# FFN up projection: x's hi and lo halves as one 512-column moving operand, gate product on GpSimd

## Chip, cores and metric

The kernel runs on one core of one Trainium2 chip. The metric is the device time of one execution in microseconds, as the median of several runs. The kernel before takes 886.51 us (3 runs, 885.42 to 887.31).

## The reference

A trunk of two decoder layers on 256 tokens of width 1024, all in float32. Each layer does token mixing (latent attention and sparse attention side by side), cross-attention into 256 memory tokens, and a gated feed-forward block (FFN) with a causal depthwise convolution, each followed by a layer norm. The change is in the FFN:

```
def conv_ffn(x, w_up, conv_w, conv_b, w_down):      # x (1,256,1024), w_up (1024, 2*2816), w_down (2816, 1024)
    u = x @ w_up
    u = causal depthwise conv of width 3 over u, + conv_b
    a, g = split(u, 2, axis=-1)
    return (a * silu(g)) @ w_down
```

## The kernel before

**Numbers as hi and lo.** TensorE multiplies in a rounded 32-bit format (float32r). To keep float32 precision every operand v is split: hi is v rounded, made by a copy on ScalarE (L130 for weights), and lo = v - hi, made by a subtraction on VectorE (L131). A product is then three matmuls accumulated in PSUM: hi·hi, hi·lo and lo·hi. Weights come in pieces of 128x1024 numbers (512 KB): SyncE starts the DMA into one of 4 "raw" buffers (L122), and the two halves go into rings of 6 "hi" and 6 "lo" buffers.

**The activation.** x lies transposed in two tiles, xTh and xTl, each [128, 2 token tiles, 8 contraction tiles, 128 tokens] (`new_xT`, L253). `transposed` (L242 to L251) fills them after each layer norm, one token tile after the other, by PE transposes into PSUM, a ScalarE copy for hi and a VectorE subtraction for lo. Cross-attention's values xv reuse the two slots (L873).

**The FFN.** The 2816 hidden columns are 22 tiles of 128 (index f), each with a part a and a gate part g. `up_piece(j)` (L925) serves f = 2j and 2j+1 for j = 0 to 10. It loads and splits four weight pieces (two for a, two for g). For each f and each part it runs `mm_tr` (L173 to L179): for each of the 8 contraction tiles three matmuls of 256 columns, with the weights stationary (hi, hi, lo) and x moving (hi, lo, hi). Both parts of an f share one PSUM bank. Then come, for each part, bias and the current tap on ScalarE (L953), two earlier taps on VectorE (L954, L955), all reading u from PSUM, and for the pair silu on ScalarE (L957), the gate product on VectorE (L958), the hi copy on ScalarE (L960) and the lo subtraction on VectorE (L961). `down_piece(f)` multiplies the result with w_down: 12 matmuls of 512 columns for one f (L970 to L972), accumulated in four PSUM banks that stay open for the whole FFN.

**Order.** The loop at L983 runs up_piece(j) and then down_piece for f = 2j-2 and 2j-1, so that the elementwise work of one pair has the next pair's up matmuls to hide behind. The last five f are summed up in a tail. In layer 1 the first j goes the "natural" way (L929 to L936): x is stationary and the weights move, token tile 0 first, while token tile 1 is still in its layer norm; the result is transposed back (L945). The framework derives all waits from the tiles' views and orders each engine's queue by its own planning; each engine runs its queue in order.

**PSUM.** Eight banks, in two groups of four: group a holds the open accumulators, group b the up results ("up") and the layer norm's transposes ("lnt"), among others.

Of the kernel before, what the change touches and what calls it, by code (L numbers as in the profile page):

```python
# [10 lines left out]
F32 = mybir.dt.float32  # L11
F32R = mybir.dt.float32r
BF16 = mybir.dt.bfloat16
AF = mybir.ActivationFunctionType
ALU = mybir.AluOpType
# [3 lines left out]
P = 128  # L19
D = 1024  # L20
S = 256
DEPTH = 2
NT = S // P
KD = D // P
# [9 lines left out]
NF = DFF // P  # L34
# [55 lines left out]
def trunk(ctx: ExitStack, tc: tile.TileContext, a: dict, out: bass.AP):  # L90
    nc = tc.nc
    V, A, G, T = nc.vector, nc.scalar, nc.gpsimd, nc.tensor
# [3 lines left out]
    big = ctx.enter_context(tc.tile_pool(name="big", bufs=1))  # L96
    tmp = ctx.enter_context(tc.tile_pool(name="tmp", bufs=2))
# [5 lines left out]
    def bank(kind):  # L103
        tag = cfg['bank'][kind]
        return ps_.tile([P, 512], F32, name=kind, tag=tag, bufs=BUFS[tag])

    def loadc(name, shape, dtype=F32):
        t = const.tile(shape, dtype, name=name, tag=name)
        nc.sync.dma_start(t, a[name])
        return t  # L110
# [4 lines left out]
    RAW, HL, PP = SIZES  # L115
# [18 lines left out]
    def wmat(w, cuts, ks=KD, cols=None, wn=None):  # L134

        n = sum(c1 - c0 for c0, c1 in cuts)
        per = max(1, 1024 // (wn or n))
        out_ = []
        for k0 in range(0, ks, per):
            k1 = min(ks, k0 + per)  # L140
            segs, o = [], 0
            for c0, c1 in cuts:
                segs.append(((0, k1 - k0), (o, o + c1 - c0),
                             w[k0 * P:k1 * P, c0:c1].rearrange("(k p) n -> p k n", p=P)))
                o += c1 - c0
            h, lo = piece(k1 - k0, n, segs, wn, cols)
            out_ += [(h[:, i], lo[:, i]) for i in range(k1 - k0)]
        return out_
# [13 lines left out]
    def split(hl, x):  # L162
        A.activation(hl[0], x, AF.Copy)
        V.tensor_tensor(hl[1], x, hl[0].bitcast(F32), op=ALU.subtract)

    def mm_nat(o, xh_, xl_, t, ws):

        for k, (h, lo) in enumerate(ws):
            T.matmul(o, xh_[:, t, k], h, start=k == 0, stop=False)  # L169
            T.matmul(o, xh_[:, t, k], lo, start=False, stop=False)  # L170
            T.matmul(o, xl_[:, t, k], h, start=False, stop=k == len(ws) - 1)  # L171

    def mm_tr(o, xh_, xl_, ws, m0):  # L173

        ms = slice(m0, m0 + P)
        for k, (h, lo) in enumerate(ws):
            T.matmul(o, h[:, ms], xh_[:, :, k], start=k == 0, stop=False)  # L177
            T.matmul(o, h[:, ms], xl_[:, :, k], start=False, stop=False)  # L178
            T.matmul(o, lo[:, ms], xh_[:, :, k], start=False, stop=k == len(ws) - 1)  # L179
# [16 lines left out]
    ident = loadc("c_ident", [P, P])  # L196
# [45 lines left out]
    def transposed(x, t, xh, xl):  # L242
        for c in range(2):
# [6 lines left out]
            A.activation(h, pv, AF.Copy)  # L250
            V.tensor_tensor(xl[:, t, 4 * c:4 * c + 4], pv, h.bitcast(F32), op=ALU.subtract)  # L251

    def new_xT():  # L253
        return [big.tile([P, NT, KD, P], F32R, name="xT" + s, tag="xT" + s) for s in "hl"]

    warm(8, 256)
    gb = []
    for i in range(2):
        gb.append([bank("fill") for _ in range(2)])
        for c in range(2):  # L260
            T.matmul(gb[i][c], ones[0:1, 0:P].bitcast(F32), rows[:, i, c * 512:(c + 1) * 512], start=True, stop=True)
    xh, xl = new_xT()
    for t in range(NT):
        layer_norm(xn[t], gb, act=cfg['lnact']['in'][t])
# [29 lines left out]
    def pcol(name, l, i, n=1):  # L294
        r0, r = PAR[name]
        c = r0 + l * r + i
        return par[:, c:c + n]
# [85 lines left out]
    for l in range(DEPTH):  # L383
# [296 lines left out]
        def ch_transposed():  # L680
            ch = new_xT()
            for k in range(5):
                pb = bank("cht")
                for t in range(NT):
                    T.transpose(pb[:, t * P:(t + 1) * P], cqn[:, t, k * P:(k + 1) * P], ident)
                gcol = pcol("cqg", l, k) if k < 3 else pcol("ckvg", l, k - 3)
                pv = pb[:, 0:S].rearrange("p (t n) -> p t n", t=NT)
                A.activation(ch[0][:, :, k], pv, AF.Copy, scale=gcol)
                V.scalar_tensor_tensor(ch[1][:, :, k], pv, gcol, ch[0][:, :, k].bitcast(F32),
                                       op0=ALU.mult, op1=ALU.subtract)  # L690
            return ch
# [134 lines left out]

        accs = proj(wout, oh, ol)
        xh, xl = new_xT()
        for t in range(NT):
            residual_ln(accs, t, gb, "1")  # L830
# [4 lines left out]
        qx, vx, pTx = {}, [], []  # L835
# [34 lines left out]

        def xa_v(i):
            if not vx:
                vx.extend(big.tile([P, NT, D], F32R, name="xv" + s, tag="xT" + s) for s in "hl")  # L873
            v, *hl = [x[:, :, i * 256:(i + 1) * 256] for x in (kvs[l].v, *vx)]
            if i in kvs[l].vwork:
                kvs[l].vwork.pop(i)(hl)
            else:
                split(hl, v)
# [23 lines left out]
        for i in range(4):  # L902
            steps[f"q{i}"] = lambda i=i: xa_q(i)
            steps[f"qk{i}"] = lambda i=i: xa_qk(i)
            steps[f"v{i}"] = lambda i=i: xa_v(i)
            steps[f"av{i}"] = lambda i=i: xa_av(i)
# [4 lines left out]
        xh, xl = new_xT()  # L911
# [13 lines left out]
        def up_piece(j):  # L925
            wsa = wmat(wup, [(j * 256, (j + 1) * 256)])
            wsg = wmat(wup, [(DFF + j * 256, DFF + (j + 1) * 256)])
            nat = []
            if j < cfg['natural']:  # L929
                nt = big.tile([P, NT, 512], F32, name="nat", tag="k1")  # L930
                for t in range(NT):
                    pb = bank("nat")
                    for s, ws in enumerate((wsa, wsg)):
                        mm_nat(pb[:, s * S:(s + 1) * S], xh, xl, t, ws)
                    A.activation(nt[:, t, :], pb, AF.Copy)
                    nat.append(nt[:, t, :])  # L936
            for i in range(2):
                f = 2 * j + i
                pb = bank("up")
                conv = []  # L940
                for s, ws in enumerate((wsa, wsg)):
                    if nat:
                        for t in range(NT):
                            c0 = s * S + t * P
                            T.transpose(pb[:, c0:c0 + P], nat[t][:, s * S + i * P:s * S + (i + 1) * P], ident)  # L945
                    else:
                        mm_tr(pb[:, s * S:(s + 1) * S], xh, xl, ws, i * P)
                for s in range(2):
                    ft = s * NF + f
                    u = pb[:, s * S:(s + 1) * S]  # L950
                    c = tmp.tile([P, S], F32, name="cv", tag=("pp", "pT")[s], bufs=(PP, 4)[s])
                    w_ = [pcol("cw", l, tap * 2 * NF + ft) for tap in range(3)]
                    A.activation(c, u, AF.Identity, bias=pcol("cb", l, ft), scale=w_[2])  # L953
                    V.scalar_tensor_tensor(c[:, 1:], u[:, :S - 1], w_[1], c[:, 1:], op0=ALU.mult, op1=ALU.add)  # L954
                    V.scalar_tensor_tensor(c[:, 2:], u[:, :S - 2], w_[0], c[:, 2:], op0=ALU.mult, op1=ALU.add)  # L955
                    conv.append(c)
                A.activation(conv[1], conv[1], AF.Silu)  # L957
                V.tensor_tensor(conv[0], conv[0], conv[1], op=ALU.mult)  # L958
                fh, fl = fr[0][:, f % KD, :], fr[1][:, f % KD, :]
                A.activation(fh, conv[0], AF.Copy)  # L960
                V.tensor_tensor(fl, conv[0], fh.bitcast(F32), op=ALU.subtract)  # L961
                down[f] = fh, fl

        def down_mm(f, w_, t, c):
# [18 lines left out]
        for j in range(NF // 2):  # L983
            up_piece(j)
            if j == 0:
                accs.update({(t, c): bank(f"acc{t}") for t in range(NT) for c in range(2)})
            for f in (2 * j - 2, 2 * j - 1):
                if 0 <= f < NF - cfg['last']:
                    down_piece(f)
# [9 lines left out]
        if l + 1 < DEPTH:  # L999
            xh, xl = new_xT()  # L1000
# [35 lines left out]
```

## Time and profile before

| | us |
|---|---|
| median of 3 runs | 886.51 (885.42 to 887.31) |
| the profiled execution | 884.51 |
| its span on the core | 882.7 |
| PE busy / VectorE / ScalarE / GpSimd | 866.8 / 660.4 / 511.2 / 39.9 |
| FFN of layer 0, of layer 1 (up matmuls first to last, plus tail) | 271 to 458, 684 to 875 |
| granted TensorE clock, mean | 0.997 |

Durations of matmuls overlap, since they are pipelined: a matmul of 256 columns is shown as 0.28 us, but the next one starts 0.12 us later. The pace is read from the start times.

### The profile page before, as it was taken

To read this page: it belongs to the slowest core of one execution; us is meant where nothing else is said; L and a number is where in the kernel's file an instruction comes from. 1 tells how busy PE (TensorE), PEld (TensorE's weight loads), DVE (VectorE), ACT (ScalarE), POOL (GpSimd) and SP (SyncE) were. 2 spreads that over 40 slices of the span, in tenths; PEclk is the share of its full clock that TensorE was granted. 3 is DMA by queue.
4 is the path that set the end of the run, shared out by engine and by line. 5 is a ranking of instruction groups with operands and counts; after the bars stand their busy time and mean duration, and the time that the engine had idled before them with its cause. 6 is when DMAs were issued, how large, how long until landed. Compare 5 with 4: busy or idle time off the path is not lost.

```text
span 882.7 us, 15902 instructions
## 1 busy us (share of the span) xinstructions
PE 866.8 (98%) x6110; PEld 798.4 (90%) x6110; DVE 660.4 (75%) x1294; ACT 511.2 (58%) x938; POOL 39.9 (5%) x60
## 2 busy tenths in 40 slices
PE   9989999999999999999999999999999999999996
PEld 6989788899989999999989998879998999999995
DVE  7799886756687777677688798858666777667767
ACT  5659764546445655465556678636573465555551
POOL 1052000000000000000000020000000000000000
PEclk9999999999999999999999999999999999999999
DMA  8953372584257556556539634546632756646631
GB/s 235 284 151 111 128 191 96 164 256 154 96 154 243 177 188 205 179 172 202 177 119 240 178 94 105 144 143 218 193 117 95 239 156 198 205 159 192 214 120 48
DMA packets 128240, 148.72 MB, mean 168 GB/s; under 512 B 6260, under 2 KB 111010, under 8 KB 128164
## 3 DMA queue, kind: packets, MB, share of 16 engines
q1 hardware_dynamic: 128159, 147.70, 54.4%
q8 instruction: 48, 0.79, 0.4%
q14 instruction: 29, 0.23, 0.1%
q10 hardware_dynamic: 4, 0.01, 0.0%
HBM read 146.64 MB, written 1.05 MB: 167 GB/s over the span
## 4 chain that ended last, share of the span: by engine, by line
PE 91%; DVE 4%; ACT 2%; DMA 1%; issue 1%; SPq 0%; POOL 0%; DVEq 0%; ACTq 0%; POOLq 0%
PE up L179 9%; PE up L178 9%; PE up L177 9%; PE acc L970 5%; PE acc L971 5%; PE acc L972 5%; PE acc L170 3%; PE acc L169 3%; PE acc L171 3%; PE fill L179 2%; PE fill L178 2%; PE xq L179 2%; PE xq L178 2%; PE xq L177 2%; PE fill L171 2%; PE fill L169 2%
## 5 line engine op out<-in xcount | busy, mean ns | idle before, releaser
L131 DVE TENSOR_TENSOR lo<-raw,hi 128x1024 fp32r<-128x1024 f32 (+5 forms) x296 | 320.2, 1094 | 81.6 <-ACT hi L130 77.2
L130 ACT ACTIVATE hi<-raw 128x1024 fp32r<-128x1024 f32 (+5 forms) x296 | 279.1, 955 | 149.7 <-PE acc L171 34.7
L179 PE MATMUL up<-xTh,lo 128*128 128x256 f32 x672 | 190.2, 283 | 0.0
L178 PE MATMUL up<-xTl,hi 128*128 128x256 f32 x672 | 190.2, 283 | 0.0
L177 PE MATMUL up<-xTh,hi 128*128 128x256 f32 x672 | 190.2, 283 | 0.0
L178 PEld LDWEIGHTS up<-xTl,hi 128*128 128x128 f32 x672 | 128.9, 192 | 0.7
L177 PEld LDWEIGHTS up<-xTh,hi 128*128 128x128 f32 x672 | 128.9, 192 | 0.7
L179 PEld LDWEIGHTS up<-xTh,lo 128*128 128x128 f32 x672 | 128.9, 192 | 0.0
L954 DVE SCALAR_TENSOR_TENSOR cv<-up,par,cv 128x255 f32<-128x255 f32 x88 | 42.0, 479 | 51.8 <-ACT cv L953 51.8
L953 ACT ACTIVATE cv<-up,par 128x256 f32<-128x256 f32 x88 | 48.8, 557 | 52.8 <-PE up L179 48.3
L971 PE MATMUL acc<-lo,frh 128*128 128x512 f32 x176 | 68.8, 391 | 0.0
L970 PE MATMUL acc<-hi,frh 128*128 128x512 f32 x176 | 68.7, 392 | 0.0
L972 PE MATMUL acc<-hi,frl 128*128 128x512 f32 x176 | 68.2, 389 | 0.0
L571 ACT ACTIVATE p<-p,nm 128x128 f32<-128x128 f32 x96 | 42.7, 447 | 9.5 <-DVE nm L568 9.2
L209 POOL TENSOR_TENSOR mv<-mv,mhalf 128x1 f32<-128x1 f32 x16 | 14.0, 875 | 647.0 <-DVE mv L233 497.1
L955 DVE SCALAR_TENSOR_TENSOR cv<-up,par,cv 128x254 f32<-128x254 f32 x88 | 41.9, 478 | 1.4
L960 ACT ACTIVATE frh<-cv 128x256 fp32r<-128x256 f32 x44 | 18.3, 417 | 37.8 <-DVE cv L958 37.7
L972 PEld LDWEIGHTS acc<-hi,frl 128*128 128x128 f32 x176 | 33.0, 188 | 7.5 <-DVE frl L961 0.6
L970 PEld LDWEIGHTS acc<-hi,frh 128*128 128x128 f32 x176 | 33.1, 188 | 7.0 <-ACT frh L960 0.8
L971 PEld LDWEIGHTS acc<-lo,frh 128*128 128x128 f32 x176 | 33.1, 188 | 6.0
L177 PE MATMUL fill<-mTh,hi 128*128 128x256 f32 x128 | 37.2, 291 | 0.0
L179 PE MATMUL fill<-mTh,lo 128*128 128x256 f32 x128 | 36.6, 286 | 0.0
(270 smaller groups left out, 2015.9 us busy)
## 6 DMA issues: line engine op xcount, KB each, us to landing
raw<-in_ffn_w_up SPq DMA_DIRECT2D x88, 512.0 KB, 4.7
raw<-in_ffn_w_down SPq DMA_DIRECT2D x44, 512.0 KB, 4.5
raw<-in_xa_wkv SPq DMA_DIRECT2D x32, 512.0 KB, 3.3
raw<-in_xa_wq SPq DMA_DIRECT2D x16, 512.0 KB, 5.2
raw<-in_xa_wo SPq DMA_DIRECT2D x16, 512.0 KB, 4.1
raw<-in_w_in SPq DMA_DIRECT2D x24, 256.0 KB, 3.7
raw<-in_w_out SPq DMA_DIRECT2D x16, 256.0 KB, 4.3
raw<-in_w_out SPq DMA_DIRECT2D x8, 512.0 KB
```

What stands on the lines that cost most here:

```text
L130: A.activation(h_, x_, AF.Copy)
L131: V.tensor_tensor(l_, x_, h_.bitcast(F32), op=ALU.subtract)
L169: T.matmul(o, xh_[:, t, k], h, start=k == 0, stop=False)
L171: T.matmul(o, xl_[:, t, k], h, start=False, stop=k == len(ws) - 1)
L177: T.matmul(o, h[:, ms], xh_[:, :, k], start=k == 0, stop=False)
L178: T.matmul(o, h[:, ms], xl_[:, :, k], start=False, stop=False)
L179: T.matmul(o, lo[:, ms], xh_[:, :, k], start=False, stop=k == len(ws) - 1)
L571: A.activation(pc[i], pc[i], AF.Exp, bias=nm[:, i:i + 1], scale=-1.0, accum_out=scs[i])
L953: A.activation(c, u, AF.Identity, bias=pcol("cb", l, ft), scale=w_[2])
L970: T.matmul(o, fh[:, ts_], h[:, cs_], start=f == 0, stop=False)
L971: T.matmul(o, fh[:, ts_], lo[:, cs_], start=False, stop=False)
L972: T.matmul(o, fl[:, ts_], h[:, cs_], start=False, stop=f == NF - 1)
```

## The change

x's tile is now one tile of [128, 8 contraction tiles, hi/lo, 2 token tiles, 128], so that hi and lo of one contraction tile lie side by side as 512 columns; the two old names are views into it. `mm_tr2` runs 8 matmuls with the hi weights and these 512 columns (left half of a full PSUM bank: hi·hi, right half: hi·lo), and then 8 with the lo weights and x's hi (256 columns) into the left half. So one part of one f takes a bank of its own, and the two halves are added up afterwards: ScalarE copies the right half into an SBUF tile u, VectorE adds the left half. The taps then read u from SBUF. The gate product and the lo subtraction go to GpSimd. All of that holds but for the last j (`late`), which stays as it was, save for the layout; layer 1's natural j = 0 keeps its matmuls, and its gate product and subtraction go to GpSimd too. The tile xv becomes one tile in the same slot.

```
+    def mm_tr2(o, x2, ws, m0):
+        ms = slice(m0, m0 + P)
+        for k, (h, lo) in enumerate(ws):
+            T.matmul(o, h[:, ms], x2[:, k], start=k == 0, stop=False)
+        for k, (h, lo) in enumerate(ws):
+            T.matmul(o[:, 0:S], lo[:, ms], x2[:, k, 0], start=False, stop=k == len(ws) - 1)
     def new_xT():
-        return [big.tile([P, NT, KD, P], F32R, name="xT" + s, tag="xT" + s) for s in "hl"]
+        xT = big.tile([P, KD, 2, NT, P], F32R, name="xT", tag="xT")
+        xTs[0] = xT
+        v = xT.rearrange("p k h t n -> p h t k n")
+        return [v[:, 0], v[:, 1]]
...
-                vx.extend(big.tile([P, NT, D], F32R, name="xv" + s, tag="xT" + s) for s in "hl")
+                v2 = big.tile([P, 2, NT, D], F32R, name="xv2", tag="xT")
+                vx.extend([v2[:, 0], v2[:, 1]])
...
+                late = j == NF // 2 - 1
+                if nat or late:
...
+                else:
+                    for s, ws in enumerate((wsa, wsg)):
+                        pb = bank("up")
+                        mm_tr2(pb, xTs[0], ws, i * P)
+                        u = tmp.tile([P, S], F32, name="u", tag=("pp", "pT")[s], bufs=(PP, 4)[s])
+                        A.activation(u, pb[:, S:2 * S], AF.Copy)
+                        V.tensor_tensor(u, pb[:, 0:S], u, op=ALU.add)
+                        us.append(u)
...
-                V.tensor_tensor(conv[0], conv[0], conv[1], op=ALU.mult)
+                E = V if late else G
+                E.tensor_tensor(conv[0], conv[0], conv[1], op=ALU.mult)
...
-                V.tensor_tensor(fl, conv[0], fh.bitcast(F32), op=ALU.subtract)
+                E.tensor_tensor(fl, conv[0], fh.bitcast(F32), op=ALU.subtract)
```

## Rows read from the trace of the kernel before

**Rows 1.** The page: TensorE's busy time, and its granted clock in 40 slices.

```profile
PE 866.8 (98%) x6110; PEld 798.4 (90%) x6110; DVE 660.4 (75%) x1294; ACT 511.2 (58%) x938; POOL 39.9 (5%) x60
PEclk9999999999999999999999999999999999999999
```

**Rows 2.** The page: the chain of waits that ended last, by engine and by line.

```profile
PE 91%; DVE 4%; ACT 2%; DMA 1%; issue 1%; SPq 0%; POOL 0%; DVEq 0%; ACTq 0%; POOLq 0%
PE up L179 9%; PE up L178 9%; PE up L177 9%; PE acc L970 5%; PE acc L971 5%; PE acc L972 5%; PE acc L170 3%; PE acc L169 3%; PE acc L171 3%; PE fill L179 2%; PE fill L178 2%; PE xq L179 2%; PE xq L178 2%; PE xq L177 2%; PE fill L171 2%; PE fill L169 2%
```

**Rows 3.** Windows, FFN stages: length, busy PE, PEld, DVE, ACT, POOL, clock, DMA, GB/s.

```profile
271.00:458.00 187.00, 187.00 (x1323) 175.97 (x1322) 135.81 (x209) 106.27 (x155) 0.92 (x1) 1.00 0.58 184
...
703.00:868.00 165.00, 165.00 (x1168) 155.30 (x1167) 119.50 (x185) 95.83 (x143) 0.00 (x0) 1.00 0.54 171
```

**Rows 4.** Windows, two periods of the FFN loop in layer 0.

```profile
356.49:390.45 33.96, 33.96 (x242) 32.04 (x241) 24.21 (x36) 19.20 (x29) 0.00 (x0) 1.00 0.60 187
```

**Rows 5.** Timeline of PE, one period: start us, duration us, line, out<-in, shape.

```profile
351.73 0.28 PE L178 MATMUL up<-xTl,hi 128*128 128x256 f32 x1
...
361.93 0.28 PE L179 MATMUL up<-xTh,lo 128*128 128x256 f32 x1
362.05 0.40 PE L970 MATMUL acc<-hi,frh 128*128 128x512 f32 x1
...
364.11 0.39 PE L970 MATMUL acc<-hi,frh 128*128 128x512 f32 x1
...
367.29 0.39 PE L972 MATMUL acc<-hi,frl 128*128 128x512 f32 x1
367.51 0.28 PE L177 MATMUL up<-xTh,hi 128*128 128x256 f32 x1
```

**Rows 6.** Groups by line and shape, same two periods: count, busy us, mean ns.

```profile
L131 DVE TENSOR_TENSOR lo<-raw,hi 128x1024 fp32r<-128x1024 f32 x12 | 14.7, 1222 | 2.9 <-ACT hi L130 2.5
...
L953 ACT ACTIVATE cv<-up,par 128x256 f32<-128x256 f32 x9 | 5.0, 558 | 7.9 <-PE up L179 7.9
...
L954 DVE SCALAR_TENSOR_TENSOR cv<-up,par,cv 128x255 f32<-128x255 f32 x8 | 3.8, 478 | 5.6 <-ACT cv L953 5.6
...
L961 DVE TENSOR_TENSOR frl<-cv,frh 128x256 fp32r<-128x256 f32 x4 | 1.7, 425 | 1.2 <-ACT frh L960 1.0
L958 DVE TENSOR_TENSOR cv<-cv 128x256 f32<-128x256 f32 x4 | 1.7, 420 | 0.0
...
L957 ACT ACTIVATE cv<-cv 128x256 f32<-128x256 f32 x4 | 1.6, 399 | 0.0
```

**Rows 7.** Groups by line and shape, GpSimd, whole trace.

```profile
L646 POOL TENSOR_TENSOR sc<-sc,c_cok 128x256 f32<-128x256 f32 x2 | 1.6, 824 | 0.0
...
L644 POOL TENSOR_TENSOR sc<-sc,cmx 128x256 f32<-128x256 f32 x2 | 1.2, 622 | 50.8 <-DVE sm L575 47.4 <-DVE cmx L642 3.4
```

**Rows 8.** Timeline of GpSimd: its longest busy stretch.

```profile
44.34 10.03 POOL L310 TENSOR_SCALAR alibi<-neg 128x256 bf16<-128x256 f32 x8 [32.20 <-DMA neg<-in_c_neg]
```

**Rows 9.** Timeline of ScalarE: two of one period's weight splits.

```profile
357.81 1.06 ACT L130 ACTIVATE hi<-raw 128x1024 fp32r<-128x1024 f32 x1 [0.75 <-PE up L178]
...
362.13 1.06 ACT L130 ACTIVATE hi<-raw 128x1024 fp32r<-128x1024 f32 x1 [0.38 <-PE up L178]
```

**Rows 10.** Groups by line and shape, VectorE, only 44.3 to 54.4 us.

```profile
L131 DVE TENSOR_TENSOR lo<-raw,hi 128x768 fp32r<-128x768 f32 x3 | 2.8, 948 | 0.0
```

**Rows 11.** Groups by line and shape, VectorE, whole trace.

```profile
L131 DVE TENSOR_TENSOR lo<-raw,hi 128x768 fp32r<-128x768 f32 x8 | 7.5, 951 | 1.0 <-ACT hi L130 1.0
```

**Rows 12.** Timeline of PE: layer 1's natural up matmuls of token tile 0.

```profile
684.48 0.39 PE L169 MATMUL nat<-hi,xTh 128*128 128x256 f32 x1 [0.76 <-ACT xTh L250]
...
691.09 1.28 PE L247 MATMUL lnt<-c_ident,x 128*128 128x128 f32 x8
```

**Rows 13.** Timeline of ScalarE: a piece split in two interleaved column halves.

```profile
473.12 1.15 ACT L130 ACTIVATE hi<-raw 128x512 fp32r<-128x512 f32 x2 [0.93 <-DMA raw<-in_w_in]
```

**Rows 14.** Timeline of VectorE: the lo halves of that piece.

```profile
473.79 1.29 DVE L131 TENSOR_TENSOR lo<-raw,hi 128x512 fp32r<-128x512 f32 x2 [0.18 <-ACT hi L130]
```

More of the change, by code (lines that the diff above doesn't have):

```diff
@@ L251, in transposed @@
             V.tensor_tensor(xl[:, t, 4 * c:4 * c + 4], pv, h.bitcast(F32), op=ALU.subtract)
+    xTs = [None]
+    def mm_tr2(o, x2, ws, m0):
[4 more added lines that the diff above has]
+            T.matmul(o[:, 0:S], lo[:, ms], x2[:, k, 0], start=False, stop=k == len(ws) - 1)
     def new_xT():
-        return [big.tile([P, NT, KD, P], F32R, name="xT" + s, tag="xT" + s) for s in "hl"]
+        xT = big.tile([P, KD, 2, NT, P], F32R, name="xT", tag="xT")
+        xTs[0] = xT
+        v = xT.rearrange("p k h t n -> p h t k n")
+        return [v[:, 0], v[:, 1]]
     warm(8, 256)
@@ L938, in up_piece @@
                 f = 2 * j + i
[L939 to L947, printed above, removed]
+                late = j == NF // 2 - 1
+                conv, us = [], []
+                if nat or late:
+                    pb = bank("up")
+                    for s, ws in enumerate((wsa, wsg)):
+                        if late:
+                            mm_tr(pb[:, s * S:(s + 1) * S], xh, xl, ws, i * P)
+                        else:
+                            for t in range(NT):
+                                c0 = s * S + t * P
+                                T.transpose(pb[:, c0:c0 + P], nat[t][:, s * S + i * P:s * S + (i + 1) * P], ident)
+                        us.append(pb[:, s * S:(s + 1) * S])
+                else:
+                    for s, ws in enumerate((wsa, wsg)):
+                        pb = bank("up")
+                        mm_tr2(pb, xTs[0], ws, i * P)
[3 more added lines that the diff above has]
+                        us.append(u)
                 for s in range(2):
                     ft = s * NF + f
-                    u = pb[:, s * S:(s + 1) * S]
+                    u = us[s]
                     c = tmp.tile([P, S], F32, name="cv", tag=("pp", "pT")[s], bufs=(PP, 4)[s])
```

## The prediction

> **What bounds the kernel now.** First the busy shares and the clock: TensorE (PE) is busy 98% of the span and its granted clock stands in the top tenth in all 40 slices [rows 1], so neither a cold clock nor one long hole is there to be won. Then the chain of waits: 91% of what ended last is PE, and the three lines of the FFN's up projection (L177 to L179) are its largest entries, 9% each [rows 2]. Shares over the whole span can mislead, so the stage itself comes next: in the FFN of layer 0 PE is busy 187.00 of 187.00 us, in that of layer 1 165.00 of 165.00, while VectorE has 135.8 and 119.5 and ScalarE 106.3 and 95.8 [rows 3]. In the FFN only PE's own pace counts, and a change is worth there what it takes from PE's instruction stream, as long as the others keep up.
>
> PE's pace has to be read from start times, since durations overlap. From 351.73 to 361.93 lie 85 steps of 256-column matmuls: 10.20/85 = 0.1200 us each. From 362.05 to 367.51 lie the 24 matmuls of 512 columns of two down pieces: 5.46/24 = 0.2275 us each [rows 5]. Doubling the columns costs 0.1075, less than another 0.12: each matmul carries 0.0125 us that does not grow with its columns. One period of the loop is then 96 x 0.12 + 24 x 0.2275 = 11.52 + 5.46 = 16.98 us; two of them are the 33.96 us of the window, in which VectorE is busy 24.21 and ScalarE 19.20 [rows 4].
>
> **The change, part by part.**
>
> *The matmuls.* The chain's largest entry changes from three matmuls per contraction tile (3 x 0.12 = 0.360) to one of 512 and one of 256 (0.2275 + 0.12 = 0.3475). That saves 0.0125 us per contraction tile: one matmul's fixed part. It applies to 10 of 11 j in layer 0 (the last is left as it is) and to 9 in layer 1 (the natural one too): 19 j x 2 f x 2 parts x 8 = 608 times, 608 x 0.0125 = 7.6 us, 0.4 us per period (16.98 to 16.58). That the columns multiplied stay the same (768 per contraction tile) is why it is so little. Bounds: the trace has no 512-column matmul with weights of w_up stationary. From below, the last 15 matmuls of the down pieces stand a little closer, (367.51 - 364.11)/15 = 0.2267 [rows 5], which gives 608 x 0.0133 = 8.1 us. From above, two of the present matmuls, 0.24, gives 0. I take 0.2275, which is the same shape and number format.
>
> *ScalarE.* Four copies of 128x256 from PSUM per period are new. Nearest rows: 0.558 us for the tap that reads PSUM (L953), 0.399 for silu from SBUF (L957) [rows 6]; I take 0.5, so 2.0 us, range 1.6 to 2.2. ScalarE goes from 19.20/2 = 9.6 to 11.6 of 16.58 us (70%). Cost on the path: nothing, hidden by PE.
>
> *VectorE.* Four adds that read PSUM are new, by L954 0.478 each, 1.9 us; by the SBUF-only L958 1.7. The gate product and the subtraction leave: 2 f x (0.420 + 0.425) = 1.7 us. The eight taps read SBUF on both sides now: between nothing gained and 8 x (0.478 - 0.420) = 0.5 us [rows 6]. So VectorE stays at 24.21/2 = 12.1 plus 0.2, less up to 0.5: about 12 of 16.58 us (73%), again beneath PE.
>
> *GpSimd.* Four two-input operations of 128x256 per period. Its rows of that shape are 0.622 and 0.824 us [rows 7]; its one-input operation on the same shape took 10.03/8 = 1.25 [rows 8]. I take 0.9, that is 3.6 us of 16.58, with 2.5 and 5.0 as ends. The path from up to down gets longer by copy, add and two slower operations: 0.5 + 0.5 + 2 x 0.5 = 2 us; down_piece for a pair comes after the next up_piece, 11.1 us of PE work later, which covers it. If that cover were gone, PE would wait 2 us in each of 19 periods, 38 us.
>
> Here one rule speaks against the change. While GpSimd ran without a break for 10 us, VectorE's two-input splits of 128x768 took 0.948 us; over the whole trace they took 0.951 [rows 8, 10, 11]: no slowing is seen. The Trainium skill ("GPSIMD Engine Reference", Specifications) has GpSimd share its SBUF interfaces with VectorE, with contention for VectorE instructions that have two SBUF inputs. By that rule the splits, and the taps as they become, would wait while GpSimd works; by the rows nothing is added to the sum.
>
> *Where weights are split.* The hi copies of a period start at 357.81 to 362.13, each when a buffer comes free [rows 9]; the next up piece starts at 367.51 [rows 5], so the first has 367.51 - 358.87 = 8.6 us in hand. In the new order a part takes 8 x 0.3475 = 2.78 us; its first hi buffer is free after 4 x 0.2275 = 0.9 us (now 4 x 0.36 = 1.4) and its first lo buffer after 1.8 + 0.5 = 2.3 us (now 1.4), so nothing comes free more than 0.9 us later. What is queued behind a late copy on ScalarE, the splits, has 8.6 us to spare. I cost it at nothing.
>
> *PSUM.* A part takes a whole bank, so group b's four banks hold two f, not four. A bank is wanted again two f later: the other part, the next f and two down pieces, 2.78 + 5.56 + 5.46 = 13.8 us after it is full, and is free after one copy and one add. Nothing.
>
> *Layout.* Merged tiles would cost if a wait on hi now also meant one on lo, or token tile 0 on token tile 1. The trace speaks against it: two interleaved halves of one buffer are copied back to back (1.15 us for both, from 473.12), though VectorE still reads the first half from 473.79 on [rows 13, 14]. So views that interleave are kept apart. The first matmul of the FFN needs lo as well as hi, but fill work lies in front.
>
> Sum: 884.51 (the profiled execution: span 882.7 plus 1.8 around it) - 7.6 = 876.9. The median of the runs shown is 2.0 above that execution, so I predict 886.51 - 7.6 = 878.9 us. What is late next: PE itself still.
>
> **Rivals.**
>
> A. *No saving in a 512-column matmul here* (the change does not do what it says). If the fixed part shows only in the down matmuls' mix, a hi matmul costs 0.24 and the time stays at 886.5. For it: no row of exactly this operand pair. Against: both shapes are the same format and run without a gap beside each other [rows 5]. The Trainium skill ("TensorE: Matmul & The Clock Gate", Back-to-back issue gap) puts the fixed part at 2.5 ns only; by it the gain would be 608 x 0.0025 = 1.5 us, an estimate, and 885 us. The trace has 12.5 ns in its place, and the measurement decides.
>
> B. *Merged tile.* Layer 1's natural matmuls of token tile 0 run from 684.48 to 691.09, before token tile 1's transposes [rows 12]. If the merged tile made them wait for tile 1, these 6.6 us would lie open: 886.5 - 7.6 + 6.6 = 885.5, no change. Against it: [rows 13, 14].
>
> C. *Part of the gain is given back* at the edges: a few periods' waits at the layers' ends and starts, or a different queue order. Two periods' worth of chain (2 us each) would leave 3.6 us: 882.9.
>
> D. *VectorE sets the pace, slower.* It gets there if GpSimd's time is taken from VectorE in full. VectorE's 12 us plus 5.0 (the upper end) is 17.0 per period, against 16.98 now: break-even. It decides from there. VectorE waits for ScalarE today in 2.5 + 5.6 us of two periods, 4 per period [rows 6]; with half of that kept, a period is 17.0 + 2 = 19.0 and 19 x 2.0 = 38 us are lost: 925. For it: the skill's rule above; against it: [rows 8, 10, 11].
>
> **How the numbers follow.** Forecast (878.9) 0.66, C 0.13, A 0.06, B 0.04, D 0.08, and 0.03 for a slower queue order of another kind. About 0.2% (1.8 us) is what a measurement can tell from no change. Faster: forecast and C, 0.79. Same: A and B, 0.10. Slower: 0.11. The range starts at 886.51 - 8.1 = 878.4, less the spread of the runs shown on either side of two medians (2 x 1.1), at 876, and reaches up over C to 885, short of A and B; that leaves out A, B, D and the other slower case, 0.21.
>
> **What would show it.** Right: PE without a gap in both FFN stages, starts of the hi matmuls 0.2275 us apart and of the lo ones 0.12, a period of 16.58 us, FFN of layer 0 shorter by 4.0 us and of layer 1 by 3.6, GpSimd at 2.5 to 5 us per period, the L131 split still at 1.22 us. Wrong: hi matmuls 0.24 apart (A); PE idle before the natural matmuls with a wait on x's tile (B); the split well above 1.22 us, or PE waiting on "hi", "lo" or an "up" bank (D).

## The result and the profile after

The changed kernel took 878.99 us (median of 4 runs, 878.50 to 879.98) against 886.08 us of the kernel before (4 runs, 885.42 to 887.31): a ratio of 0.9927, 95% interval 0.9915 to 0.9939. The forecast was 878.9. Run again later it took 880.11 us, ratio 0.9950 (0.9931 to 0.9969), 5.2 us less than the kernel before beside it.

The page after, TensorE's line and its clock (answers to [rows 1]):

```profile
PE 860.3 (98%) x5502; PEld 766.7 (87%) x5502; DVE 665.2 (76%) x1290; ACT 532.5 (61%) x1014; POOL 132.4 (15%) x140
...
PEclk9989999999999999999999999999999999999998
```

608 matmuls are gone (6110 to 5502), and PE's busy time fell by 6.5 us while its share stayed at 98%. GpSimd went from 39.9 to 132.4 us. The chain of waits after (answers to [rows 2]):

```profile
PE 91%; DVE 4%; ACT 2%; DMA 2%; issue 1%; POOL 0%; SPq 0%; DVEq 0%; ACTq 0%; POOLq 0%
PE up L259 16%; PE up L261 8%; PE acc L996 5%; PE acc L997 5%; PE acc L998 5%; PE acc L170 3%; PE acc L171 3%; PE acc L169 3%; PE fill L178 2%; PE fill L179 2%; PE xq L179 2%; PE xq L178 2%; PE xq L177 2%; PE fill L171 2%; PE fill L169 2%; PE fill L170 2%
```

The three up lines of 9% each became one of 16% (512 columns) and one of 8% (256 columns). The bound is where it was. The FFN stages and two periods of the loop, in windows (columns as in [rows 3, 4]):

```profile
275.00:455.90 180.90, 180.90 (x990) 156.98 (x989) 136.84 (x208) 116.34 (x193) 47.13 (x41) 1.00 0.59 186
703.00:863.00 160.00, 160.00 (x879) 139.10 (x879) 119.81 (x178) 103.46 (x176) 46.01 (x40) 1.00 0.54 173
350.42:383.64 33.22, 33.22 (x177) 28.68 (x176) 24.84 (x37) 21.71 (x37) 9.46 (x8) 1.00 0.61 194
```

PE has no gap in these windows; a period is 33.22/2 = 16.61 us, where [rows 4] gave 16.98. PE's timeline over one period (start us, duration us, line, tiles, shape), which answers to [rows 5]:

```profile
350.42 1.98 PE L259 MATMUL up<-xT,hi 128*128 128x512 f32 x8
352.23 1.11 PE L261 MATMUL up<-xT,lo 128*128 128x256 f32 x8
353.18 2.00 PE L259 MATMUL up<-xT,hi 128*128 128x512 f32 x8
355.02 1.11 PE L261 MATMUL up<-xT,lo 128*128 128x256 f32 x8
...
361.56 0.40 PE L996 MATMUL acc<-hi,frh 128*128 128x512 f32 x1
...
367.03 1.98 PE L259 MATMUL up<-xT,hi 128*128 128x512 f32 x8
```

Eight hi matmuls take 1.81 to 1.84 us by their starts (0.226 to 0.230 each), eight lo ones 0.95 to 0.96 (0.119 to 0.120). A part is (361.56 - 350.42)/4 = 2.785 us, where three 256-column matmuls per tile took 8 x 0.36 = 2.88.

Read by starts, layer 0's stage (first up matmul to last down matmul) went from 271.09-457.85 to 272.76-455.97: 186.76 to 183.21 us. Layer 1's, from the first natural matmul, went from 684.48-874.73 to 683.02-869.86: 190.25 to 186.84. Together 6.96 us are saved. The two profiled executions differ by only 884.51 - 879.98 = 4.5 us, chiefly because the first cross-attention query matmul, ahead of all changed matmuls, started at 187.67 in the one and at 189.34 in the other; over all kernels profiled here it lies between 187.5 and 190.7. Near 48 us PE waits once on VectorE, for 2.6 us in the one and 3.2 in the other, and the granted clock between 40 and 60 us is 0.91 and 0.83. So stages tell more here than spans.

What became of the other engines, in groups over the same two periods (busy us, mean ns | idle before, releaser), beside [rows 6]:

```profile
L131 DVE TENSOR_TENSOR lo<-raw,hi 128x1024 fp32r<-128x1024 f32 x13 | 16.2, 1260 | 4.8 <-ACT hi L130 4.8
...
L130 ACT ACTIVATE hi<-raw 128x1024 fp32r<-128x1024 f32 x12 | 12.4, 1045 | 0.0
...
L984 POOL TENSOR_TENSOR cv<-cv 128x256 f32<-128x256 f32 x4 | 5.7, 1417 | 21.7 <-PE up L259 14.0 <-ACT cv L982 7.7
...
L979 DVE SCALAR_TENSOR_TENSOR cv<-u,par,cv 128x255 f32<-128x255 f32 x8 | 3.8, 479 | 3.0 <-ACT cv L978 3.0
L987 POOL TENSOR_TENSOR frl<-cv,frh 128x256 fp32r<-128x256 f32 x4 | 3.8, 947 | 2.1 <-ACT frh L986 2.1
L971 DVE TENSOR_TENSOR u<-up,u 128x256 f32<-128x256 f32 x8 | 3.3, 417 | 0.4 <-ACT u L970 0.4
...
L970 ACT ACTIVATE u<-up 128x256 f32<-128x256 f32 x8 | 3.0, 373 | 2.4 <-PE up L261 2.4
```

ScalarE's queue shows how much room is left. In [rows 6] its first tap (L953) stood waiting on PE for 7.9 us in two periods, and its weight copies waited for PE to free a buffer:

```profile
L130 ACT ACTIVATE hi<-raw 128x1024 fp32r<-128x1024 f32 x12 | 12.7, 1058 | 5.1 <-PE up L178 3.0 <-PE acc L972 2.0
```

Together that is 13.0 us, 6.5 per period. Now the copy out of PSUM (L970), which has taken the first tap's place, waits on PE for 2.4, 1.2 per period, and the weight copies no longer wait. Time in which an engine waits on the one that sets the pace is taken here as its slack: ScalarE is busy 21.71/33.22 = 65%, but has 1.2 us of slack in 16.61, since the rest of its idle time goes into waits on VectorE and GpSimd.

### The profile page after: what moved, and what is told of

It reads as the page before. It is cut to its first block, busy times and chain, and to the rows that moved or that the text cites. A ratio compares the mean times of both kernels' runs of the same rounds, so it can differ in the third digit from the quotient of the medians.

```text
span 877.9 us, 14948 instructions
## 1 busy us (share of the span) xinstructions
PE 860.3 (98%) x5502; PEld 766.7 (87%) x5502; DVE 665.2 (76%) x1290; ACT 532.5 (61%) x1014; POOL 132.4 (15%) x140
## 4 chain that ended last, share of the span: by engine, by line
PE 91%; DVE 4%; ACT 2%; DMA 2%; issue 1%; POOL 0%; SPq 0%; DVEq 0%; ACTq 0%; POOLq 0%
PE up L259 16%; PE up L261 8%; PE acc L996 5%; PE acc L997 5%; PE acc L998 5%; PE acc L170 3%; PE acc L171 3%; PE acc L169 3%; PE fill L178 2%; PE fill L179 2%; PE xq L179 2%; PE xq L178 2%; PE xq L177 2%; PE fill L171 2%; PE fill L169 2%; PE fill L170 2%
## 5 line engine op out<-in xcount | busy, mean ns | idle before, releaser
L130 ACT ACTIVATE hi<-raw 128x1024 fp32r<-128x1024 f32 (+5 forms) x296 | 275.8, 951 | 108.9 <-PE acc L171 34.4
L259 PE MATMUL up<-xT,hi 128*128 128x512 f32 x608 | 152.1, 392 | 0.0
L259 PEld LDWEIGHTS up<-xT,hi 128*128 128x128 f32 x608 | 110.3, 189 | 20.3
L261 PEld LDWEIGHTS up<-xT,lo 128*128 128x128 f32 x608 | 82.9, 190 | 5.9
L984 POOL TENSOR_TENSOR cv<-cv 128x256 f32<-128x256 f32 x40 | 54.2, 1356 | 218.7 <-ACT cv L982 170.0
L261 PE MATMUL up<-xT,lo 128*128 128x256 f32 x608 | 84.8, 282 | 0.0
L978 ACT ACTIVATE cv<-u,par 128x256 f32<-128x256 f32 x76 | 45.4, 598 | 49.6 <-DVE u L971 49.6
L979 DVE SCALAR_TENSOR_TENSOR cv<-u,par,cv 128x255 f32<-128x255 f32 x76 | 37.6, 495 | 26.4 <-ACT cv L978 26.4
L987 POOL TENSOR_TENSOR frl<-cv,frh 128x256 fp32r<-128x256 f32 x40 | 38.0, 952 | 20.3 <-ACT frh L986 20.3
L980 DVE SCALAR_TENSOR_TENSOR cv<-u,par,cv 128x254 f32<-128x254 f32 x76 | 37.9, 498 | 2.5
```

The lines of the kernel that those rows point to most:

```text
L130: A.activation(h_, x_, AF.Copy)
L259: T.matmul(o, h[:, ms], x2[:, k], start=k == 0, stop=False)
L261: T.matmul(o[:, 0:S], lo[:, ms], x2[:, k, 0], start=False, stop=k == len(ws) - 1)
L984: E.tensor_tensor(conv[0], conv[0], conv[1], op=ALU.mult)
```

## The experiments

The main theory: the gain is the fixed part of 608 matmuls, and nothing else in the change moves the time. Rivals: the move to GpSimd, or the merged layout, holds part of it; or the new work costs something that the gain covers. Ratios are against the kernel before, run beside them (medians 885.07 us for E1 to E4, 884.52 for E5 to E8, 885.35 for F1 to F4).

**E1. Product and subtraction back on VectorE** (edit of the changed kernel).

```
-                E = V if late else G
+                E = V
```

> The changed kernel, but gate product and lo subtraction stay on VectorE in every j. Theory (only PE's per-matmul fixed part, 608 x 0.0125 us, is the gain; GpSimd's part is worth nothing): 879.0 us like the changed kernel, ratio to the kernel before 0.992; VectorE goes from 12.4 to about 14 of 16.6 us per period, no gap on PE. Rival (the move to GpSimd is what lets VectorE keep up): PE waits on weights or on an up bank, 882 us or more.

880.34 us, 0.9938 (0.9919 to 0.9957); FFN stages 183.19 and 186.82 us, the changed kernel's to 0.02. VectorE is at 26.60 of 33.22 us and GpSimd idle. So the move to GpSimd was worth nothing.

**E2. Only that move, in the kernel before.**

```
+                E = V if j == NF // 2 - 1 else G
-                V.tensor_tensor(conv[0], conv[0], conv[1], op=ALU.mult)
+                E.tensor_tensor(conv[0], conv[0], conv[1], op=ALU.mult)
```

(and the same for the subtraction)

> The kernel before, with only the gate product and the lo subtraction on GpSimd (not in the last j). Theory: nothing that PE waits for changes, 886.1 us, ratio 1.000. Rival (relief of VectorE is part of the gain): some us faster, 884 or less. Rival (GpSimd and VectorE hold each other up): slower, splits of the weights above 1.22 us and PE waiting.

885.22 us, 0.9998 (0.9988 to 1.0008); stages 186.85 and 190.28 against 186.76 and 190.25. Nothing here either.

**E3. The hi matmul of 512 as two of 256** for seven of eight contraction tiles: the order, layout and engines stay changed, only 532 matmuls come back.

```
-            T.matmul(o, h[:, ms], x2[:, k], start=k == 0, stop=False)
+            if k == 0:
+                T.matmul(o, h[:, ms], x2[:, k], start=True, stop=False)
+            else:
+                T.matmul(o[:, 0:S], h[:, ms], x2[:, k, 0], start=False, stop=False)
+                T.matmul(o[:, S:2 * S], h[:, ms], x2[:, k, 1], start=False, stop=False)
```

> The changed kernel with the 512-column hi matmul cut into its two 256-column halves for seven of the eight contraction tiles (the first keeps 512): same order, same layout, same evictions, 532 matmuls more. Theory (fixed part per matmul): 532 x 0.0125 = 6.7 us come back, 879.0 + 6.7 = 885.7. Rival (the gain comes from order, layout or the new evictions): stays at 879.

884.91 us, 0.9997 (0.9986 to 1.0008): the gain is gone. Three hi matmuls of its PE timeline:

```profile
353.46 0.28 PE L263 MATMUL up<-xT,hi 128*128 128x256 f32 x1
353.58 0.28 PE L262 MATMUL up<-xT,hi 128*128 128x256 f32 x1
353.70 0.29 PE L263 MATMUL up<-xT,hi 128*128 128x256 f32 x1
```

They stand 0.12 us apart, as in [rows 5]. The stages grew by 3.35 + 3.16 = 6.51 us, 12.2 ns for each of the 532.

**E4. The lo matmul of 256 as two of 128**, 608 more matmuls, same columns.

```
+            for t in range(NT):
+                T.matmul(o[:, t * P:(t + 1) * P], lo[:, ms], x2[:, k, 0, t], ...)
```

> The changed kernel with each 256-column lo matmul cut into two of 128 columns (608 matmuls more, with a weight load each). Theory (a fixed 13 ns per matmul beside columns/2.4): 0.067 us each, 608 x 0.013 = 8 us more, 887. Rival (0.12 us is the least that one weight load with its matmul can take, whatever the columns): 608 x 0.12 = 73 us more, 952.

943.73 us, 1.0655 (1.0635 to 1.0674). The stages are 217.19 and 217.45 us, 64.6 more, or 106 ns for each of the 608. Its PE timeline, one part:

```profile
352.82 2.07 PE L259 MATMUL up<-xT,hi 128*128 128x512 f32 x8
354.72 1.90 PE L262 MATMUL up<-xT,lo 128*128 128x128 f32 x16
356.46 0.91 PE L259 MATMUL up<-xT,hi 128*128 128x512 f32 x3
```

16 matmuls of 128 columns take 1.74 us, 0.109 each, hardly less than the 0.12 of twice the columns. The fixed part read at 256 and 512 columns does not carry down to 128, where the theory had 0.067; what sets 0.109 there no run here shows.

**E5. Only the merged layout, in the kernel before** (rival B).

```
+        xT = big.tile([P, KD, 2, NT, P], F32R, name="xT", tag="xT")
+        v = xT.rearrange("p k h t n -> p h t k n")
+        return [v[:, 0], v[:, 1]]
```

(and the same for the natural x, `xv2`)

> The kernel before with only the new layout: x's hi and lo in one tile and xv in one tile, matmuls and everything else as before. Theory (the layout changes no wait): 885 us as before, ratio 1.000. Rival (merged tile): token tile 0's natural matmuls of layer 1 wait for token tile 1, or a slot frees later, up to 6.6 us more, 892. Rival (the layout is part of the gain): 882 or less.

885.38 us, 1.0007 (0.9997 to 1.0017); stages 186.81 and 190.26. The layout costs and gives nothing.

**E6. GpSimd's two operations doubled**, each copy just ahead of or behind the real one, into a scratch tile that nobody reads (not in the last j).

```
+                    G.tensor_tensor(jk6, conv[0], conv[1], op=ALU.mult)
                 E.tensor_tensor(conv[0], conv[0], conv[1], op=ALU.mult)
 ...
+                    G.tensor_tensor(jk6, conv[0], fh.bitcast(F32), op=ALU.subtract)
```

> The changed kernel with both GpSimd operations of each f done a second time into a scratch tile that nobody reads, 80 operations more: GpSimd goes from 4.7 to about 9 us per period. Theory (PE's pace alone counts, the rest has room): 879 us, as the changed kernel; VectorE's busy time grows by its slowed splits (1.33 instead of 1.22 us) to some 13 of 16.6 us. Rival (GpSimd takes VectorE's time and VectorE sets the pace): every period grows, 5 us of GpSimd more per period against 4 us of room, 19 x 1 us = 19 us or more, 898.

934.10 us, 1.0563 (1.0544 to 1.0582): some 55 us lost. A window of layer 0's FFN, then PE's waits in it (line, waited for: us, times, longest):

```profile
300.00:460.00 160.00, 149.90 (x790) 127.65 (x790) 106.61 (x148) 86.83 (x149) 66.57 (x69) 0.97 0.52 165
```

```profile
PE up L259 <- ACT hi L130: 8.1, 5, 2.0
...
```

VectorE is busy 67%, ScalarE 54%, GpSimd 42%: no engine is full, and PE waits all the same, on the hi halves of weights. ScalarE's timeline tells why:

```profile
361.86 0.42 ACT L989 ACTIVATE frh<-cv 128x256 fp32r<-128x256 f32 x1 [2.07 <-POOL cv L987]
362.18 1.04 ACT L130 ACTIVATE hi<-raw 128x1024 fp32r<-128x1024 f32 x1
...
381.34 0.42 ACT L989 ACTIVATE frh<-cv 128x256 fp32r<-128x256 f32 x1 [2.06 <-POOL cv L987]
```

The hi copy of the product (L989) stands 2.07 us for GpSimd, and the weights' hi copy, which needs nothing of GpSimd, stands behind it. ScalarE's round is 381.34 - 361.86 = 19.48 us, where PE needs 16.61. Around the first of PE's waits, 2.0 us up to 355.55, its granted clock is 0.91 (340 to 360 us), after 1.00 from 300 to 340. Two explanations were left: this queue, or contention between GpSimd and VectorE, whose splits took up to 1.76 us here. F1 and F4 tell them apart.

**E7. The last j in the new form too.** `if nat:` instead of `if nat or late:`.

> The changed kernel with the last j's up matmuls in the new form as well (product and subtraction still on VectorE there). Theory for the matmuls: 64 x 0.0125 = 0.8 us less. Against it stands a longer path behind the last up matmul (copy and add, about 0.8 us) in front of the tail's down matmuls: if that path is open, nothing is won or up to 1 us is lost a layer. Expected 878.5 to 879.5, too close to tell from the changed kernel by time; PE's idle time in the tail is what tells.

880.21 us, 0.9952 (0.9940 to 0.9965). The stages are 183.43 and 187.98, 0.22 and 1.14 us longer than the changed kernel's. PE's waits at the end of layer 1:

```profile
PE acc L993 <- ACT frh L983: 0.7, 1, 0.7
PE acc L995 <- DVE frl L984: 0.3, 1, 0.3
```

In the last j no up piece lies ahead of the down pieces to cover the longer path through copy and add: the 0.8 us that 64 matmuls fewer should give is lost there, and 1.4 us more.

**E8. Cross-attention's queries and keys in the new form too.** Each group of 128 output columns (index m) gets its own bank and `mm_tr2`, then copy, add and split, as in the FFN; the memory's two tiles become one, laid out as x's.

> The changed kernel with the same form of matmul in two more places: the query projection of cross-attention and its key projection of the memory, 128 + 128 contraction tiles. Theory (fixed part per matmul): 256 x 0.0125 = 3.2 us less than the changed kernel, 876, ratio 0.989. Rival (those stages end on other waits: softmax, layer norm, more work on ScalarE and VectorE for the added halves): no gain or a loss of some us.

881.24 us (878.93 to 883.38), 0.9954 (0.9937 to 0.9971). From the first query matmul to the first up matmul it took 82.32 us against 83.42, and in layer 1 71.30 against 71.96: 1.8 us less, where 3.2 were expected. The time of the whole does not show it. PE's waits between 60 us and the first query matmul are longer than in the changed kernel, 4.8 us against 1.2, on tiles of the softmax beside which the keys are projected (pT, 3.0 us, and nm, 1.8). F3, without the keys, has 1.2 again. So for the keys the rival in the expectation holds, as far as one profile of each kernel can show.

**F1. Two extra GpSimd operations per f again, but both behind the subtraction**, where ScalarE doesn't wait for them (not in the last j).

```
+                    for _ in range(2):
+                        G.tensor_tensor(jk6, conv[0], fh.bitcast(F32), op=ALU.subtract)
```

> The changed kernel with two more GpSimd operations per f into a scratch tile, both behind the lo subtraction, where nobody waits for them: GpSimd as busy as in the run with both operations doubled, the path from gate product to hi copy as in the changed kernel. Theory (that run lost 55 us because ScalarE stood in its queue waiting for the longer gate product, with weight copies behind it): 879 to 881 us. Rival (GpSimd's busy time itself takes SBUF access from VectorE): 930 us again.

893.90 us, 1.0113 (1.0090 to 1.0136): 14 us more than F2, about a quarter of E6's loss. Two waits of ScalarE over layer 0's FFN, first the changed kernel, then F1:

```profile
ACT cv L978 <- DVE u L971: 21.5, 27, 1.8
...
ACT u L970 <- PE up L261: 11.8, 17, 1.4
```

```profile
ACT cv L978 <- DVE u L971: 34.1, 27, 2.7
...
ACT u L970 <- PE up L261: 2.7, 2, 1.4
```

And VectorE's groups of F1 between 300 and 420 us:

```profile
L131 DVE TENSOR_TENSOR lo<-raw,hi 128x1024 fp32r<-128x1024 f32 x43 | 57.0, 1338 | 14.6 <-ACT hi L130 14.6
L980 DVE SCALAR_TENSOR_TENSOR cv<-u,par,cv 128x254 f32<-128x254 f32 x28 | 16.5, 590 | 0.9
L979 DVE SCALAR_TENSOR_TENSOR cv<-u,par,cv 128x255 f32<-128x255 f32 x27 | 14.3, 530 | 10.3 <-ACT cv L978 10.3
```

Taps and splits are slower beside GpSimd (0.530 and 0.590 against 0.48, 1.338 against 1.260), ScalarE waits longer for VectorE's add, and its slack against PE is used up. Two product copies one period apart:

```profile
355.74 0.42 ACT L986 ACTIVATE frh<-cv 128x256 fp32r<-128x256 f32 x1 [1.25 <-POOL cv L984]
...
372.98 0.42 ACT L986 ACTIVATE frh<-cv 128x256 fp32r<-128x256 f32 x1 [1.25 <-POOL cv L984]
```

ScalarE's round takes 372.98 - 355.74 = 17.24 us against PE's 16.61, 0.63 more. Weights split ahead cover that for most of a layer, and the lag comes due at its end. Two windows of layer 0 (columns as in [rows 3]) and PE's longest wait:

```profile
272.00:416.00 144.00, 144.00 (x771) 124.47 (x770) 112.18 (x153) 90.21 (x154) 73.03 (x65) 1.00 0.58 183
451.00:454.00 3.00, 3.00 (x8) 2.33 (x8) 1.39 (x3) 1.29 (x3) 0.00 (x0) 0.50 0.87 286
```

```profile
PE acc L1000 <- ACT frh L986: 3.2, 1, 3.2
```

Up to 416 us PE has no gap. Then it waits 0.8 and 0.3 us for lo halves and 3.2 us for a product copy of the last j, and behind that wait its granted clock is 0.50, the lower level (1.2 GHz). Layer 0's stage is 190.06 - 183.21 = 6.8 us longer, layer 1's 196.53 - 186.84 = 9.7.

**F2. The changed kernel once more**, to stand beside F1, F3 and F4.

> The changed kernel once more, unaltered, on the chip of this call, as the measure for the others: ratio to the kernel before 0.993, within 0.991 to 0.995.

880.11 us (878.79 to 883.26); stages 183.23 and 186.84, as in the first profile.

**F3. Only the queries in the new form too** (E8 without the keys).

> The changed kernel with the new form of matmul in the query projection of cross-attention only, 128 contraction tiles. Theory (fixed part per matmul): 128 x 0.0125 = 1.6 us less than the changed kernel, read from the stretch from the first query matmul to the first up matmul, which was 83.42 and 71.96 us in the two layers. Rival (the softmax behind it ends last): no gain, or a loss.

878.53 us (876.92 to 878.85), 0.9923 (0.9905 to 0.9941), the lowest of F1 to F4, though its interval overlaps F2's. The two stretches from queries to FFN are 82.75 and 71.28 us against 83.42 and 71.98: 1.4 us less (1.6 expected), as the same fixed part would give.

**F4. E6, with the hi copy of the product on GpSimd**: more GpSimd work than E6, but ScalarE no longer waits for GpSimd.

```
-                A.activation(fh, conv[0], AF.Copy)
+                G.tensor_copy(fh, conv[0])            (except in the last j)
```

> The run with both GpSimd operations doubled, and the hi copy of the product moved from ScalarE to GpSimd as well (not in the last j): GpSimd even busier, 11 us per period, its path longer, but ScalarE no longer waits for GpSimd. Theory (ScalarE's queue): the 55 us vanish, 879 to 882 us. Rival (GpSimd's load or its path): 934 us or more.

884.33 us, 0.9991 (0.9978 to 1.0004): 50 us of E6's loss are gone. Layer 0, window:

```profile
300.00:420.00 120.00, 120.00 (x637) 103.67 (x637) 103.56 (x133) 73.55 (x117) 80.39 (x75) 1.00 0.62 195
```

GpSimd is at 67% and VectorE at 86%, both far above E6, and PE has no gap: the stage is 183.21 us, as in the changed kernel. What E6 lost was lost in ScalarE's queue; that F4 also takes two copies of 0.42 us per round off ScalarE is less than the 2.9 us by which E6's round was too long. Layer 1 took 191.50, 4.7 us more than the changed kernel, all of it in the first round of the loop. There a down matmul waits 2.2 us on GpSimd's copy, and the eight matmuls behind the wait run at a granted clock of about 0.5:

```profile
714.63:718.13 3.50, 3.50 (x8) 2.62 (x9) 3.50 (x4) 0.42 (x1) 3.32 (x4) 0.52 0.76 250
```

They take 3.50 us, where eight take 8 x 0.2275 = 1.82 in [rows 5].

## Why the prediction was right

*The matmuls* were the step that carried it, and it held. The sum was 608 x 0.0125 = 7.6 us; the stages gave 6.96. Layer 0's stage became 3.55 us shorter (4.0 forecast), layer 1's 3.41 (3.6). The rest is in the part: 2.785 us instead of 2.78, and the down pieces 367.03 - 361.56 = 5.47 instead of 5.46, which makes a period 16.61 instead of 16.58; over 19 periods 0.03 is the 0.6 us. E3 shows the cause: with the matmuls back and all else changed, the time is that of before. Each matmul that is gone took a weight load with it (PEld x6110 to x5502), and each that E3 puts back brings one, so the runs show the fixed part of the pair and not which of the two it belongs to. E1, E2 and E5 show that the other two parts of the change give nothing. The median came out at 878.99 beside a forecast of 878.9, and that it is so close is luck: between these two medians lie 7.1 us and in F2 5.2, while the stages give 6.96 and 6.94.

*Rival A*, no saving at 512 columns, is out by the starts of 0.226 to 0.230. The Trainium skill ("TensorE: Matmul & The Clock Gate", Back-to-back issue gap) gives its 2.5 ns for a matmul by itself, without its weight load. In this stream every matmul has a load, and E3's 12.2 ns decide, as [rows 5] did. *Rival B* is out by E5. *Rival C*, waits at the edges, is out too: PE waits nowhere in layer 0's stage, before or after, and in layer 1's twice, at the natural matmuls and as long after as before (L169 on ScalarE's half of x's tile 0.8 us, L171 on VectorE's 0.5).

*The small prices* were off in both directions and covered either way: the PSUM copy 0.373 us (0.5 priced), the add 0.417 (0.478), the taps 0.479 and 0.483 out of SBUF (no gain of the 0.5 us per period that was the upper end), the first tap 0.598 (L978; 0.558 before). VectorE came to 24.84/2 = 12.4 us per period (12), ScalarE to 10.9 (11.6), GpSimd to 4.7 (3.6, with 2.5 and 5.0 as ends).

*Where weights are split* held for the change itself, but one sentence of it was read too widely: "What is queued behind a late copy on ScalarE, the splits, has 8.6 us to spare. I cost it at nothing." Six lines from around one period of the changed kernel (DMA issues, ScalarE, VectorE, PE):

```profile
361.06 0.34 SPq L122 DMA_DIRECT2D raw<-in_ffn_w_down  x1
362.74 8.60 SPq L122 DMA_DIRECT2D raw<-in_ffn_w_up  x4
361.98 1.05 ACT L130 ACTIVATE hi<-raw 128x1024 fp32r<-128x1024 f32 x1
368.64 1.04 ACT L130 ACTIVATE hi<-raw 128x1024 fp32r<-128x1024 f32 x1
369.71 1.23 DVE L131 TENSOR_TENSOR lo<-raw,hi 128x1024 fp32r<-128x1024 f32 x1 [2.03 <-ACT hi L130]
380.93 0.39 PE L996 MATMUL acc<-hi,frh 128*128 128x512 f32 x1
```

The copies follow the order of loading, in each period four pieces of w_up and then two of w_down. The copy of 361.98 is the last of the four for the up matmuls that start at 367.03. It ends at 363.03, and its tiles are first wanted in the second half of the part that starts at 369.80, at 369.80 + 0.91 = 370.7: 7.7 us in hand. The copy of 368.64, which stands behind a hi copy that waited for GpSimd, belongs to w_down: its split ends at 370.94, the last of the four issues follows at 370.97 into the raw buffer that has come free, and with four such buffers in turn this piece was loaded four issues earlier, at 361.06. It is the second w_down piece of the period and is wanted at 380.93. So the lead of some 8 us was still there. But a lead is spent once, while a round that is longer than PE's takes from it every time. What ScalarE has to spare in each round is its wait on PE, 1.2 us, down from 6.5, and the prediction did not ask for it. F1, 0.63 us per round too long, used the lead up over a layer; E6, 2.9 us too long, had PE waiting from 353.6 us on, in every period.

*"No slowing is seen"* was wrong for two-input operations. Splits and GpSimd operations of the changed kernel (VectorE, then GpSimd):

```profile
349.85 1.22 DVE L131 TENSOR_TENSOR lo<-raw,hi 128x1024 fp32r<-128x1024 f32 x1
359.81 1.22 DVE L131 TENSOR_TENSOR lo<-raw,hi 128x1024 fp32r<-128x1024 f32 x1
361.34 1.37 DVE L131 TENSOR_TENSOR lo<-raw,hi 128x1024 fp32r<-128x1024 f32 x1
```

```profile
350.52 1.14 POOL L984 TENSOR_TENSOR cv<-cv 128x256 f32<-128x256 f32 x1 [3.83 <-ACT cv L982]
352.19 0.74 POOL L987 TENSOR_TENSOR frl<-cv,frh 128x256 fp32r<-128x256 f32 x1 [0.53 <-ACT frh L986]
359.94 1.69 POOL L984 TENSOR_TENSOR cv<-cv 128x256 f32<-128x256 f32 x1 [7.00 <-PE up L259]
```

In these rows the operation that starts while the other engine's runs is the one that takes longer. The products of 350.52 and 359.94 started within a split and took 1.14 and 1.69 us, while these splits kept their 1.22; the split of 361.34 started within a product and took 1.37. Alone, the subtraction of 352.19 took 0.74. Had the later one stood until the other ended, these three would have taken 0.55 + 0.74 = 1.29, 1.09 + 0.74 = 1.83 and 0.29 + 1.22 = 1.51 us; each took 0.14 or 0.15 less. Over the whole trace 157 splits of 128x1024 without one of these GpSimd operations beside them took 1.220 us on average, 37 in which one started 1.218, and 34 that started during one 1.354. [Rows 8, 10, 11] had a one-input operation on GpSimd and could not show this for two-input ones. The Trainium skill's rule ("GPSIMD Engine Reference", Specifications), that VectorE instructions with two SBUF inputs contend with GpSimd, agrees with these rows and with F1, and the prediction gave it too little weight. *Rival D* was right that GpSimd's work can turn the gain into a loss, and wrong about the place: not VectorE full (F4 has it at 86% and loses nothing in layer 0), but ScalarE's queue waiting for GpSimd (E6), and to a lesser part ScalarE waiting for a slowed VectorE (F1).

## What to carry to other kernels

Where PE runs without a gap, count matmul instructions as well as columns: here one of 512 columns in place of two of 256 saved some 12 ns, and cutting one of 256 into two of 128 cost 106 ns. Read the slack of the other engines from how long they wait on the engine that sets the pace, round by round, not from their busy shares: here 65% busy meant 1.2 us of slack in 16.6. A lead, such as weights split 8 us ahead, is no slack: it hides a round that is too long only until it is spent. Keep a hop to a slow engine out of the in-order queue that also feeds PE, or move the waiting instruction to the slow engine itself, as F4 did.

## What was not expected of the hardware

- A matmul of 128 columns with its own weight load took 0.109 us, one of 256 columns 0.12 (E4, [rows 5]): half the columns hardly shorten it.
- An operation of VectorE with two tensor inputs on 128x255 took 0.479 us with both in SBUF and 0.478 with one in PSUM ([rows 6] and the groups above): the copy out of PSUM buys nothing for the taps.
- Of a VectorE split and a GpSimd operation with two inputs that overlap, the one that starts second takes longer, nearly as if it stood until the first ended: GpSimd's on 128x256 0.74 us alone (the subtraction at 352.19) and up to 1.69 (the product at 359.94), the split 1.22 alone and 1.37 (at 361.34).
- Behind a wait of PE of 2 to 3 us its granted clock stood at about 0.5 for some 3 us (F1 from 451 us, F4 from 714.63 us), so a wait cost more than its length.
